# The end of a mixture-of-experts layer: only the last expert is split, in two halves, and TensorE adds the last shift of one token block

## The chip, the cores and the metric

The kernel runs on one core of one Trainium2 chip. The core has five engines with their own queues: TensorE (PE; its weight loads are listed apart as PEld), VectorE (DVE), ScalarE (ACT), GpSimd (POOL) and SyncE (SP), which here issues the transfers. The metric is the device time of one execution in microseconds, median of several; lower is better. TensorE's clock has two levels, 1.2 and 2.4 GHz, shown as a granted clock of 0.5 and 1.0.

## The reference

One transformer layer over 256 latent tokens of 1024 channels: a mixer (attention and pooling), a layer norm, and then the part that matters here, a mixture of 32 experts in 4 groups, two experts per token:

```python
for g in range(N_GROUPS):
    a = jnp.einsum('td,edf->tef', ht, w_gate[sl])
    u = jnp.einsum('td,edf->tef', ht, w_up[sl])
    act = jax.nn.silu(a) * u * gates[:, sl, None]
    y = y + jnp.einsum('tef,efd->td', act, w_down[sl])
...
h_new = layer_norm(alpha * h_new + gate2 * y, ln2_g, ln2_b)
```

All is float32. Each expert has a gate and an up matrix of 1024 x 512 and a down matrix of 512 x 1024, 2 MB each, 6 MB per expert.

## The kernel before

**Weights.** From about 190 us on the kernel streams the 32 experts through 20 slots of 1 MB in SBUF, taken in a fixed round (`wtile`, line 867). SP issues one transfer after the other (line 877 for gate and up in four, line 886 for down in two); a slot's new transfer waits until the products that read the old tile are done. Load calls run two experts ahead.

**One expert.** Up to 32 tokens of an expert stand as 32 columns. `gate_up` (line 816) multiplies them by gate and up, 8 steps `k` of 8 products into one PSUM tile `gue`; ACT takes the SiLU (line 827), DVE multiplies (line 833), and `turn` (line 836) transposes to `aTe`. `down` (line 841) makes 16 products of 256 columns into `ye`, and DVE multiplies by `g2b` into the expert's 32 rows of `yp` (line 850). This runs inside the next expert's `gate_up`, ahead of its step 2. Four experts fill the 128 rows of `yp`; then four products of 512 columns with `OTg` (`close_group`) add the rows to the tokens in `ya`, four PSUM tiles: two token blocks by two column halves. Each product of the program stands as two MATMUL records in the trace.

**Order.** Tile's scheduler may move instructions, except where `tc.keep_in_program_order` pins them: `pin` does that for products while `pinned[0]` is set, `fx` for others.

**The end before.** The last two experts, 30 and 31, are treated apart (`last_two`, line 960). Both experts' gate and up come first, then both down matrices in eight pieces of 256 columns, 512 KB each (`PIECES`, `parts`), interleaved so that pieces of 30 run ahead of those of 31. The layer norm's rows `l2` are loaded after all of that (line 1012), and POOL spreads them to all partitions (line 942). After gate and up of expert 31, `piece` (line 1047) makes 16 products of 64 columns and four DVE multiplications per piece; `gather` (line 1060) adds 256 finished columns to both token blocks, and a finished half gets its statistics (line 1066). Then, per token block i and half d (lines 1088 to 1116): `first` subtracts the mean and multiplies by the norm's gain; `second` scales by the reciprocal deviation and adds the shift, for block 0 by ACT and POOL (lines 1096, 1097), for block 1 by one DVE instruction (line 1099); four transfers of 256 KB write the result (line 1103).

Of the kernel before, what the change touches and what calls it, by code (L numbers as in the profile page):

```python
# [8 lines left out]
F32 = mybir.dt.float32  # L9
# [12 lines left out]
NE = 32  # L22
# [5 lines left out]
EPS = 1e-5  # L28
NEG = -1e30
WINS = (2, 4, 8, 16)  # L30
PIECES = ((0, 256, 512, 768, 1024), (0, 256, 512, 768, 1024))


@with_exitstack
def block_kernel(ctx, tc, x, cx, cols, rows, gate_bias, bands, w_mod, w_in, bias, w_grp, w_attn, w_pool, w_out,
# [14 lines left out]
    def two(name):  # L50
        return ps.tile([P, 512], F32, tag="two", bufs=2, name=name)

    def tmpb(name):
        return ps.tile([P, 512], F32, tag="tmp", bufs=2, name=name)
# [9 lines left out]
    def fx(ins):  # L64
        return tc.keep_in_program_order(ins) if early[0] else ins
# [709 lines left out]
    def mm(*a, **k):  # L775
        return pin(nc.tensor.matmul(*a, **k))  # L776
# [90 lines left out]
    def wtile(shape, name):  # L867
        r, t = order[slot[0] % 20]
        slot[0] += 1
        return r.tile(shape, F32, tag=t, name=name)  # L870

    def load_gate_up(e):
        ts = []
        for q in range(4):
            t = wtile([P, 4, 512], f"wgu{e}_{q}")
            w = (w_gate, w_up)[q % 2]
            nc.sync.dma_start(t, w[e].rearrange("(a p b) f -> a p b f", a=2, b=4)[q // 2])
            ts.append(t)
        return lambda k: [ts[k // 4 * 2 + s][:, k % 4, :] for s in range(2)]
# [65 lines left out]
    def first_residual():  # L945
        r = wtile([P, 2, D], "res")
        l1 = two_rows(2, "l1")
        for i in range(2):
# [4 lines left out]
            V.scalar_tensor_tensor(o, l1[:, 1], ALPHA, o, op0=OP.mult, op1=OP.add)  # L953
        return r

    parts = sorted(((i, a, b) for i in range(2) for a, b in zip(PIECES[i], PIECES[i][1:])),
                   key=lambda t: (t[1] // 256 + t[0] * 1.5, t[1]))
    loaded, groups, acts, outs = {}, {}, {}, {}

    def last_two(e):  # L960
        for i in range(2):
            loaded[e + i] = (load_gate_up(e + i), {})
        for i, a, b in parts:
            wds = loaded[e + i][1]
            if a % 512 == 0:
                wds[a // 512] = wtile([P, 4, 512], f"wd{e + i}_{a // 512}")
            nc.sync.dma_start(wds[a // 512][:, :, a % 512:a % 512 + b - a],
                              w_down[e + i].rearrange("(p k) f -> p k f", k=4)[:, :, a:b])

    def load_ahead(e):  # L970
        if e < NE - 2:
            loaded[e] = (load_gate_up(e), load_down(e))
        elif e == NE - 2:
            last_two(e)

    def open_group(g):
        outs[g] = (spread_back(groups[g][1], 0, P, f"g{g}"), M.tile([P, D], F32, tag="yp", bufs=1, name=f"yp{g}"))
# [29 lines left out]
    for e in range(NE):  # L1007
        if e == OV - 1:
            res = first_residual()
        load_ahead(e + 2)  # L1010
        if e == NE - 4:
            l2 = two_rows(4, "l2")
        last = e >= NE - 2
        pinned[0] = e < 1 or last
        g, j = e // EG, e % EG

        def mid(k):
            if e == 0 and k % 2 == 0:
                step(k // 2)
            if e - 1 in acts_in and e - 1 < NE - 2 and k == 2:  # L1020
                old_work(e - 1)
            if e == NE - 1 and k == 2:
                acts[e - 1] = turn(acts_in.pop(e - 1), f"e{e - 1}")

        acts_in[e] = gate_up(groups[g][0], CAP * j, loaded[e][0], f"e{e}", mid)
        if j == EG - 2 and e < NE - EG and e != OV - 1:
            dispatch_next(g + 1)
        if e == OV:
            old_work(e)
            most = nc.values_load(cnt[0:1, NE:NE + 1], min_val=0, max_val=T)  # L1030
            with tc.If(most > CAP):
                was, pinned[0] = pinned[0], False
                overflow()
                pinned[0] = was
            dispatch_next(g + 1)
        if e == OV + 1:
            for i in range(2):
                for d in range(2):
                    mm(ya[i][d], lhsT=ident, rhs=res[:, i, 512 * d:512 * d + 512], start=False,
                                     stop=False)  # L1040
# [2 lines left out]
    OT, yp = outs[NE // EG - 1]  # L1043
    fx = tc.keep_in_program_order
    stats = [M.tile([P, 2, 6], F32, name=f"fst{i}", bufs=1) for i in range(2)]

    def piece(n, e, c, w):
        y = (two, tmpb)[n // 2 % 2](f"yl{n}")
        wd = loaded[NE - 2 + e][1][c // 512]
        for f in range(4):  # L1050
            for d in range(4):
                o = c % 512 + w * d
                mm(y[32 * d:32 * d + 32, 0:w], lhsT=acts[NE - 2 + e][:, f, :], rhs=wd[:, f, o:o + w],
                   start=f == 0, stop=f == 3)
        p = 64 + 32 * e
        for d in range(4):
            o = slice(c + w * d, c + w * d + w)
            fx(V.tensor_mul(yp[p:p + 32, o], y[32 * d:32 * d + 32, 0:w], g2b[32 * d:32 * d + 32, o]))  # L1058

    def gather(c0, c1):  # L1060
        for i in range(2):
            t = ya[i][c0 // 512]
            mm(t[:, c0 % 512:c0 % 512 + c1 - c0], lhsT=OT[:, P * i:P * i + P], rhs=yp[:, c0:c1], start=False,
               stop=c1 % 512 == 0)
            if c1 % 512 == 0:
                fx(V.bn_stats(stats[i][:, c0 // 512, :], t))  # L1066

    ready = []
    for n, (i, a, b) in enumerate(parts):
        piece(n, i, a, (b - a) // 4)  # L1070
        if n == 0:
            acts[NE - 1] = turn(acts_in.pop(NE - 1), f"e{NE - 1}")
        while ready:
            gather(*ready.pop(0))
        if i:
            ready.append((a, b))
    gather(*ready.pop(0))
    l2g, l2b = l2[:, 0], l2[:, 1]


    fin = keep.tile([P, 2, D], F32, tag="k16", name="fin")
# [1 line left out]
    for i in range(2):  # L1083
# [1 line left out]
        fx(V.bn_aggr(mv[:, 0:2], flat(stats[i])))  # L1085
        nc.scalar.activation(mv[:, 2:3], mv[:, 1:2], AF.Sqrt, bias=epst, scale=1.0)
        mvs.append(mv)
    def first(i, d):
        cs = slice(512 * d, 512 * d + 512)
        fx(V.scalar_tensor_tensor(fin[:, i, cs], ya[i][d], mvs[i][:, 0:1], l2g[:, cs], op0=OP.subtract, op1=OP.mult))  # L1090

    def second(i, d):
        cs = slice(512 * d, 512 * d + 512)
        f = fin[:, i, cs]
        if i == 0:
            fx(nc.scalar.activation(f, f, AF.Copy, scale=mvs[i][:, 3:4]))
            fx(nc.gpsimd.tensor_add(f, f, l2b[:, cs]))
        else:
            fx(V.scalar_tensor_tensor(f, f, mvs[i][:, 3:4], l2b[:, cs], op0=OP.mult, op1=OP.add))

    def write(i, d):
        cs = slice(512 * d, 512 * d + 512)
        fx(nc.sync.dma_start(out[P * i:P * i + P, cs], fin[:, i, cs]))

    for i in range(2):
        for d in range(2):
            first(i, d)
            if d == 0:
                fx(V.reciprocal(mvs[i][:, 3:4], mvs[i][:, 2:3]))
            if i == 0:  # L1110
                second(i, d)
    for d in range(2):
        second(1, d)
    for d in range(2):
        for i in range(2):
            write(i, d)


# [57 lines left out]
```

## Time and profile before

| | |
|---|---|
| median of 3 runs | 732.76 us (732.16 to 733.72) |
| profiled execution | 733.38 us, its span 731.7 us |
| busy in the span | PE 78%, PEld 59%, DVE 43%, ACT 21%, POOL 2% |
| mean granted TensorE clock | 0.867 |
| moved by DMA | 260.09 MB, mean 355 GB/s |

The span runs from the first to the last instruction; times in rows are microseconds from its start. The page gives the span in 40 slices of 18.3 us. From slice 18 to 38 the DMA digit is 9 and the rate 415 to 420 GB/s; the last two slices have 311 and 70 GB/s. A row "[0.71 <-DMA wd...]" says that the engine stood idle for 0.71 us and what ended that; "issue" is idle time that ended with nothing the profile shows.

### The profile page before, as it was taken

How to read it: one execution, taken by the hardware profiler on the slowest of the kernel's cores; microseconds unless marked ns; L12 is line 12 of the kernel's file. 1: busy time of each engine (PE TensorE's matmuls, PEld its weight loads, DVE VectorE, ACT ScalarE, POOL GpSimd, SP SyncE). 2: the span in 40 equal slices, each digit the busy share in tenths (PEclk: the TensorE clock that was granted, in tenths of full speed). 3: DMA queues.
4: the chain of work that ended last, by engine and by line, in shares of the span. 5: the costliest groups of instructions: out<-in, count | busy, mean ns of one | idle time of the engine just before them, and what ended most of it. 6: DMA issues, size and time to landing. Idle time of an engine off the chain costs nothing.

```text
span 731.7 us, 16776 instructions
## 1 busy us (share of the span) xinstructions
PE 570.9 (78%) x7373; PEld 429.5 (59%) x7374; DVE 316.5 (43%) x778; ACT 156.1 (21%) x305; POOL 17.4 (2%) x39
## 2 busy tenths in 40 slices
PE   7898999999999989885767756668576659757462
PEld 5787666599997757664355434446334427634341
DVE  5669947979658554332122113112112332312126
ACT  4333455555545441010000001001000001100011
POOL 1000000000000030000000000000000010000003
PEclk9999999999999969997876869777785787979788
DMA  9999764789987749999999999999999999999991
GB/s 292 309 347 386 270 176 158 265 312 349 354 309 312 261 157 385 416 417 418 419 418 420 417 419 420 417 418 417 419 417 419 420 415 417 416 418 419 418 311 70
DMA packets 69628, 260.09 MB, mean 355 GB/s; under 512 B 6568, under 2 KB 27560, under 8 KB 45228
## 3 DMA queue, kind: packets, MB, share of 16 engines
q1 hardware_dynamic: 69550, 258.97, 90.9%
q8 instruction: 59, 0.97, 0.5%
q14 instruction: 19, 0.16, 0.1%
HBM read 257.90 MB, written 1.05 MB: 354 GB/s over the span
## 4 chain that ended last, share of the span: by engine, by line
DMA 52%; issue 36%; PE 8%; DVE 3%; POOL 0%; DVEq 0%; ACT 0%; SPq 0%; POOLq 0%
DMA wgu<-in_w_expert_up_dram 28%; DMA wd<-in_w_expert_down_dram 17%; DMA wgu<-in_w_expert_gate_dram 8%; PE gue L776 4%; PE ye L776 1%; PE pdd L776 1%; PE ya L776 1%; DVE yp L1058 0%; DVE se L684 0%; PE yl L776 0%; DVE fst L1066 0%; DVEq L1172 0%; DVE fin L1090 0%; DVE eq L684 0%; DVE spe L833 0%
## 5 line engine op out<-in xcount | busy, mean ns | idle before, releaser
L776 PE MATMUL gue<-wgu,xgd 128*32 128x128 f32 x4096 | 173.3, 329 | 82.5 <-DMA wgu<-in_w_expert_up_dram 52.5
L776 PEld LDWEIGHTS gue<-wgu,xgd 128*32 128x32 f32 x4096 | 138.5, 132 | 120.1 <-DMA wgu<-in_w_expert_up_dram 63.8
L776 PE MATMUL ye<-wd,aTe 128*32 128x256 f32 x960 | 73.3, 435 | 32.7 <-DVE aTe L838 15.7
L850 DVE TENSOR_TENSOR yp<-ye,g2b 32x256 f32<-32x256 f32 x120 | 50.4, 420 | 100.1 <-PE ye L776 98.7
L833 DVE TENSOR_TENSOR spe<-gue,sie 128x128 f32<-128x128 f32 x32 | 12.0, 375 | 161.8 <-ACT sie L827 161.6
L827 ACT ACTIVATE sie<-gue 128x128 f32<-128x128 f32 x32 | 8.9, 277 | 335.6 <-PE gue L776 335.6
L776 PEld LDWEIGHTS ye<-wd,aTe 128*32 128x32 f32 x960 | 32.4, 121 | 60.8 <-issue 17.7
L776 PE MATMUL pdd<-OHd,hx 128*128 128x128 f32 x256 | 41.7, 315 | 3.4 <-DVE yp L850 3.0
L776 PEld LDWEIGHTS pdd<-OHd,hx 128*128 128x128 f32 x256 | 37.0, 223 | 11.7 <-issue 5.8
L776 PE MATMUL ya<-yp,OTg 128*128 128x512 f32 (+1 forms) x72 | 33.4, 598 | 7.1 <-DVE yp L850 5.2
L362 DVE SCALAR_TENSOR_TENSOR ms<-wr,sil,ms 128x512 f32<-128x512 f32 x42 | 36.9, 878 | 0.2
L806 DVE TENSOR_SCALAR xgd<-pdd,G2c,B2c 128x128 f32<-128x128 f32 x32 | 13.1, 410 | 48.3 <-PE pdd L776 48.1
L804 ACT ACTIVATE xgd<-pdd,B2c,G2c 128x128 f32<-128x128 f32 x32 | 14.6, 457 | 84.3 <-DVE xgd L806 80.7
L776 PEld LDWEIGHTS ya<-yp,OTg 128*128 128x128 f32 x72 | 12.7, 199 | 22.4 <-DVE yp L850 13.2
L414 ACT ACTIVATE sb<-sb,mx 128x512 f32<-128x512 f32 x16 | 11.5, 719 | 10.3 <-DVE mx L413 10.1
L859 DVE COPY OTg<-potg 128x256 f32<-128x256 f32 x8 | 3.4, 424 | 23.0 <-PE ya L776 14.0
L423 PE MATMUL ptt<-ident,sb 128*128 128x128 f32 x64 | 10.2, 284 | 2.9 <-DVE yaT L69 2.7
L423 PEld LDWEIGHTS ptt<-ident,sb 128*128 128x128 f32 x64 | 6.8, 140 | 7.2 <-DVE yaT L69 5.3
L469 PEld LDWEIGHTS po<-pT,kv 128*64 128x64 f32 x128 | 7.4, 136 | 5.6 <-issue 3.3
L838 DVE STREAM_TRANSPOSE aTe<-spe 128x128 f32<-128x128 f32 x32 | 10.0, 312 | 1.1
L942 POOL PARTITION_BROADCAST l<-l1r x4 | 2.8, 798 | 318.3 <-DMA l1r<-in_rows_dram 318.3
L400 PE MATMUL s<-kv,qT 64*128 64x512 f32 x32 | 10.1, 640 | 0.3 <-DVE mx L412 0.3
(851 smaller groups left out, 971.4 us busy)
## 6 DMA issues: line engine op xcount, KB each, us to landing
wgu<-in_w_expert_gate_dram SPq DMA_DIRECT2D x64, 1024.0 KB, 19.9
wgu<-in_w_expert_up_dram SPq DMA_DIRECT2D x64, 1024.0 KB, 20.5
wd<-in_w_expert_down_dram SPq DMA_DIRECT2D x60, 1024.0 KB, 19.9
wr<-in_w_mod_dram SPq DMA_DIRECT2D x16, 1024.0 KB, 6.6
wm<-in_w_mod_dram SPq DMA_DIRECT2D x16, 512.0 KB, 7.9
wg<-in_w_in_dram SPq DMA_DIRECT2D x8, 1024.0 KB
wq<-in_w_in_dram SPq DMA_DIRECT2D x8, 512.0 KB, 8.3
wo<-in_w_out_dram SPq DMA_DIRECT2D x4, 1024.0 KB, 8.8
```

The source lines that it names most:

```text
L362: V.scalar_tensor_tensor(o, v, sil[:, k + j, 0:1], o, op0=OP.mult, op1=OP.add)
L400: ins = nc.tensor.matmul(ss[r], lhsT=qT[hr, c, P * tt:P * tt + P], rhs=kT[hr, c, :], start=True, stop=True)
L414: nc.scalar.activation(sb, sb, AF.Exp, bias=mx[:, 2:3], scale=1.0, accum_out=mx[:, 3:4])
L423: nc.tensor.transpose(pt[:, P * j:P * j + P], sb[:, P * j:P * j + P], ident)
L469: ins = nc.tensor.matmul(po[64 * r:64 * r + 64, 0:P], lhsT=vr[:, j, 128 * m + 64 * r:128 * m + 64 * r + 64], rhs=pTs[i - 1 + r][:, j, :], ...
L776: return pin(nc.tensor.matmul(*a, **k))
L804: nc.scalar.activation(xg[:, k, :], src, AF.Identity, bias=B2c[:, k:k + 1], scale=G2c[:, k:k + 1])
L806: V.tensor_scalar(xg[:, k, :], src, G2c[:, k:k + 1], B2c[:, k:k + 1], op0=OP.mult, op1=OP.add)
L827: nc.scalar.activation(si, gu[:, 0, :], AF.Silu)
L833: V.tensor_mul(sp.rearrange("p (k r) -> p k r", k=4), by_four(gu[:, 1, :]), by_four(si))
L838: V.transpose(flat(aT), si)
L850: V.tensor_mul(yp[32 * par:32 * par + 32, 256 * d:256 * d + 256], y[32 * d:32 * d + 32, 0:256], g2b[32 * d:32 * d + 32, 256 * d:256 * d + ...
```

## The change

Expert 30 loses its special treatment: its down matrix comes in the usual two transfers, ahead of gate and up of expert 31, and its down products run inside `gate_up` of expert 31. It is no longer pinned. Expert 31's down matrix comes in two halves of 512 columns, 1 MB each (`load_last`); per half there are 16 products of 128 columns, four DVE multiplications, and products of 512 columns into both token blocks. The rows `l2` are loaded ahead of expert 30. For token block 0 a product of `ident` with the shift fills a PSUM tile `fo` early (`shift`); at the end a diagonal matrix `dg` of the reciprocal deviations, made by ACT, multiplies the half into the same tile, and ACT copies it out. POOL no longer takes part at the end. One line less at the head of the file moves all line numbers by one.

```diff
-    def last_two(e):
-        for i in range(2):
-            loaded[e + i] = (load_gate_up(e + i), {})
-        for i, a, b in parts:
...
+    def load_last(e):
+        gu, ts = load_gate_up(e), []
+        for d in range(2):
+            t = wtile([P, 4, 512], f"wd{e}_{d}")
+            nc.sync.dma_start(t, w_down[e].rearrange("(p k) f -> p k f", k=4)[:, :, 512 * d:512 * d + 512])
+            ts.append(t)
+        return gu, ts
...
-        load_ahead(e + 2)
         if e == NE - 4:
             l2 = two_rows(4, "l2")
-        last = e >= NE - 2
+        load_ahead(e + 2)
+        last = e == NE - 1
...
+    fos = [two(f"fo{d}") for d in range(2)]
+    def shift(d):
+        fx(nc.tensor.matmul(fos[d], lhsT=ident, rhs=l2b[:, 512 * d:512 * d + 512], start=True, stop=False))
+    def gather(d):
+        for i in range(2):
+            mm(ya[i][d], lhsT=OT[:, P * i:P * i + P], rhs=yp[:, 512 * d:512 * d + 512], start=False, stop=True)
+            fx(V.bn_stats(stats[i][:, d, :], ya[i][d]))
+    aT = turn(acts_in.pop(NE - 1), f"e{NE - 1}")
+    for h in range(2):
+        y = tmpb(f"yl{h}")
+        shift(h)
+        wd = loaded[NE - 1][1][h]
+        for f in range(4):
             for d in range(4):
...
+                mm(y[32 * d:32 * d + 32, 0:P], lhsT=aT[:, f, :], rhs=wd[:, f, P * d:P * d + P], start=f == 0,
+                   stop=f == 3)
...
+        gather(h)
...
-            fx(nc.scalar.activation(f, f, AF.Copy, scale=mvs[i][:, 3:4]))
-            fx(nc.gpsimd.tensor_add(f, f, l2b[:, cs]))
...
+                    fx(nc.scalar.activation(dg, ident, AF.Copy, scale=mvs[0][:, 3:4]))
+                fx(nc.tensor.matmul(fos[d], lhsT=dg, rhs=part(0, d), start=False, stop=True))
...
+        fx(nc.scalar.copy(part(0, d), fos[d]))
```

SP's queue at the end, before: `wgu` are gate and up, of expert 31 in the first four rows; `wd_0_7710` and `wd_1_7715` are the down matrix of expert 30, `wd_0_7713` and `wd_1_7719` that of 31.

```order
L877 DMA wgu_0_7702<-in_w_expert_gate_dram 128x2048
L877 DMA wgu_1_7704<-in_w_expert_up_dram 128x2048
L877 DMA wgu_2_7706<-in_w_expert_gate_dram 128x2048
L877 DMA wgu_3_7708<-in_w_expert_up_dram 128x2048
L967 DMA wd_0_7710<-in_w_expert_down_dram 128x4x256 x2
L967 DMA wd_0_7713<-in_w_expert_down_dram 128x4x256
L967 DMA wd_1_7715<-in_w_expert_down_dram 128x4x256
L967 DMA wd_0_7713<-in_w_expert_down_dram 128x4x256
L967 DMA wd_1_7715<-in_w_expert_down_dram 128x4x256
L967 DMA wd_1_7719<-in_w_expert_down_dram 128x4x256 x2
L938 DMA l2r<-in_rows_dram 1x2048
```

The same place of the change: `wd_0_7709` and `wd_1_7711` are the down matrix of expert 30, then gate and up of 31, and its two halves.

```order
L885 DMA wd_0_7709<-in_w_expert_down_dram 128x2048
L885 DMA wd_1_7711<-in_w_expert_down_dram 128x2048
L876 DMA wgu_0_7809<-in_w_expert_gate_dram 128x2048
L876 DMA wgu_1_7811<-in_w_expert_up_dram 128x2048
L876 DMA wgu_2_7813<-in_w_expert_gate_dram 128x2048
L876 DMA wgu_3_7815<-in_w_expert_up_dram 128x2048
L961 DMA wd_0_7817<-in_w_expert_down_dram 128x4x512
L961 DMA wd_1_7819<-in_w_expert_down_dram 128x4x512
```

The 2 MB of expert 30's down matrix moved from behind to ahead of expert 31's gate and up; `l2r` stands further up, ahead of expert 30.

TensorE's queue from the end of expert 31's gate and up to its last product, before (`yl` are the pieces; with `aTe_8032` of expert 30, with `aTe_8109` of 31):

```order
L776 MATMUL gue_8015<-wgu_3_7708,xgd_7543 32x128 x4
L776 MATMUL yl_8088<-wd_0_7710,aTe_8032 32x64 x16
L776 MATMUL yl_8111<-wd_0_7710,aTe_8032 32x64 x16
L776 MATMUL yl_8132<-wd_0_7713,aTe_8109 32x64 x16
L776 MATMUL yl_8153<-wd_1_7715,aTe_8032 32x64 x16
L776 MATMUL ya_2868<-yp_7849,OTg_7847 128x256
L776 MATMUL ya_2870<-yp_7849,OTg_7847 128x256
L776 MATMUL yl_8176<-wd_0_7713,aTe_8109 32x64 x16
L776 MATMUL yl_8197<-wd_1_7715,aTe_8032 32x64 x16
L776 MATMUL ya_2868<-yp_7849,OTg_7847 128x256
L776 MATMUL ya_2870<-yp_7849,OTg_7847 128x256
L776 MATMUL yl_8222<-wd_1_7719,aTe_8109 32x64 x16
```

The same place of the change, to the end:

```order
L775 MATMUL gue_8011<-wgu_3_7815,xgd_7543 32x128 x4
L1043 MATMUL fo_8105<-l_7695,ident 128x512
L775 MATMUL yl_8109<-wd_0_7817,aTe_8107 32x128 x16
L775 MATMUL ya_2868<-yp_7845,OTg_7843 128x512
L775 MATMUL ya_2870<-yp_7845,OTg_7843 128x512
L1043 MATMUL fo_8106<-l_7695,ident 128x512
L775 MATMUL yl_8135<-wd_1_7819,aTe_8107 32x128 x16
L775 MATMUL ya_2869<-yp_7845,OTg_7843 128x512
L775 MATMUL ya_2871<-yp_7845,OTg_7843 128x512
L1086 MATMUL fo_8105<-fin,dg 128x512
L1086 MATMUL fo_8106<-fin,dg 128x512
```

The second half's products now stand behind the first half's products into `ya` and behind the second fill; expert 30's down products left this place.

They stand in the middle of expert 31's gate and up, in the change (`ye_8030`):

```order
L775 MATMUL gue_8011<-wgu_0_7809,xgd_7543 32x128 x4
L775 MATMUL gue_8011<-wgu_1_7811,xgd_7543 32x128 x4
L775 MATMUL gue_8011<-wgu_0_7809,xgd_7543 32x128 x4
L775 MATMUL gue_8011<-wgu_1_7811,xgd_7543 32x128 x4
L775 MATMUL ye_8030<-wd_0_7709,aTe_8028 32x256 x8
L775 MATMUL ye_8030<-wd_1_7711,aTe_8028 32x256 x8
L775 MATMUL gue_8011<-wgu_0_7809,xgd_7543 32x128 x4
L775 MATMUL gue_8011<-wgu_1_7811,xgd_7543 32x128 x4
```

Before, expert 29's down products stood at this place of expert 30, and none in expert 31; in the change those of 29 stand ahead of all of expert 30's.

## Rows read from the trace of the kernel before

**Rows 1.** The page, shares of the span in the chain that ended last.
```profile
DMA 52%; issue 36%; PE 8%; DVE 3%; POOL 0%; DVEq 0%; ACT 0%; SPq 0%; POOLq 0%
```
**Rows 2.** Timeline of SP: start, us, line, transfer, count.
```profile
678.11 0.33 SPq L877 DMA_DIRECT2D wgu<-in_w_expert_up_dram  x1
681.42 0.33 SPq L877 DMA_DIRECT2D wgu<-in_w_expert_gate_dram  x1
683.74 0.33 SPq L877 DMA_DIRECT2D wgu<-in_w_expert_up_dram  x1
686.25 22.82 SPq L967 DMA_DIRECT2D wd<-in_w_expert_down_dram  x8
```
**Rows 3.** The down tiles from 640 us: issue duration min/median/max in ns.
```profile
L967 SPq DMA_DIRECT2D wd<-in_w_expert_down_dram x8: 541/1358/8861, 686.2 to 707.7; - x8
```
**Rows 4.** Stretches: length, busy time by engine, then granted clock, DMA share, GB/s.
```profile
58.00:78.00 20.00, 18.09 (x135) 14.49 (x134) 18.78 (x47) 7.81 (x15) 0.00 (x0) 1.00 1.05 387
640.00:690.00 50.00, 26.89 (x514) 18.35 (x518) 7.52 (x19) 0.83 (x3) 0.00 (x0) 0.83 1.01 419
704.50:712.00 7.50, 5.89 (x186) 5.08 (x187) 3.70 (x16) 1.56 (x2) 0.00 (x0) 0.79 1.01 323
```
**Rows 5.** Timeline of TensorE: start, us, product, records, idle before and its releaser.
```profile
661.67 3.74 PE L776 MATMUL ya<-yp,OTg 128*128 128x512 f32 x8 [0.29 <-DVE yp L850]
688.72 1.51 PE L776 MATMUL gue<-wgu,xgd 128*32 128x128 f32 x24 [1.75 <-DMA wgu<-in_w_expert_up_dram]
690.00 3.64 PE L776 MATMUL ye<-wd,aTe 128*32 128x256 f32 x32
693.41 3.07 PE L776 MATMUL gue<-wgu,xgd 128*32 128x128 f32 x96
699.46 1.98 PE L776 MATMUL gue<-wgu,xgd 128*32 128x128 f32 x56 [1.99 <-DMA wgu<-in_w_expert_up_dram]
704.46 3.21 PE L776 MATMUL gue<-wgu,xgd 128*32 128x128 f32 x56 [1.86 <-DMA wgu<-in_w_expert_up_dram]
715.71 0.63 PE L776 MATMUL yl<-wd,aTe 128*32 128x64 f32 x26 [2.02 <-issue]
```
**Rows 6.** One-us stretches where the granted clock changed (third number from the end).
```profile
693.00:694.00 1.00, 1.00 (x20) 0.74 (x16) 0.29 (x1) 0.00 (x0) 0.00 (x0) 0.51 1.05 434
707.00:708.00 1.00, 1.00 (x48) 0.95 (x37) 0.00 (x0) 0.26 (x1) 0.00 (x0) 0.69 0.98 295
724.00:725.00 1.00, 0.00 (x0) 0.00 (x0) 1.00 (x2) 1.00 (x2) 0.30 (x1) 0.85 0.00 0
```
**Rows 7.** Timeline of all engines at the end.
```profile
707.74 0.28 ACT L827 ACTIVATE sie<-gue 128x128 f32<-128x128 f32 x1 [10.90 <-PE gue L776]
708.46 0.31 DVE L838 STREAM_TRANSPOSE aTe<-spe 128x128 f32<-128x128 f32 x1
722.64 0.28 DVE L1085 BATCH_NORM_AGGREGATE fmv<-fst 128x2 f32<-128x12 f32 x2
723.83 1.37 ACT L1096 ACTIVATE fin<-fin,fmv 128x512 f32<-128x512 f32 x2 [0.46 <-DVE fmv L1109]
```
**Rows 8.** DVE from 690 us, shapes apart: count, busy us, mean ns, idle before.
```profile
L1058 DVE TENSOR_TENSOR yp<-yl,g2b 32x64 f32<-32x64 f32 x32 | 7.1, 222 | 3.3 <-PE yl L776 2.9
L1066 DVE BATCH_NORM_STATS2 fst<-ya 128x6 f32<-128x512 f32 x4 | 2.6, 691 | 0.8 <-PE ya L776 0.8
L850 DVE TENSOR_TENSOR yp<-ye,g2b 32x256 f32<-32x256 f32 x4 | 1.7, 419 | 12.8 <-PE ye L776 12.8
```
**Rows 9.** The output's tiles: ns min/median/max, first and last start.
```profile
L1099 DVE SCALAR_TENSOR_TENSOR fin<-fin,fmv,l x2: 787/1266/1746, 725.7 to 726.4; 128x512 f32<-128x512 f32 x2
L1103 SPq DMA_DIRECT2D out_dram<-fin x4: 332/336/374, 726.0 to 728.2; - x4
```
**Rows 10.** Stretches of 1 us while the result is written.
```profile
727.00:728.00 1.00, 0.00 (x0) 0.00 (x0) 1.00 (x1) 0.00 (x0) 0.64 (x1) 0.50 1.04 391
729.00:730.00 1.00, 0.00 (x0) 0.00 (x0) 0.00 (x0) 0.00 (x0) 0.00 (x0) 0.50 0.91 342
```

More of the change, by code (lines that the diff above doesn't have):

```diff
@@ L30 @@
 WINS = (2, 4, 8, 16)
-PIECES = ((0, 256, 512, 768, 1024), (0, 256, 512, 768, 1024))
 @with_exitstack
@@ L954, in first_residual @@
         return r
-    parts = sorted(((i, a, b) for i in range(2) for a, b in zip(PIECES[i], PIECES[i][1:])),
-                   key=lambda t: (t[1] // 256 + t[0] * 1.5, t[1]))
     loaded, groups, acts, outs = {}, {}, {}, {}
-    def last_two(e):
-        for i in range(2):
-            loaded[e + i] = (load_gate_up(e + i), {})
-        for i, a, b in parts:
[L964 to L968, printed above, removed]
+    def load_last(e):
[5 more added lines that the diff above has]
+        return gu, ts
     def load_ahead(e):
-        if e < NE - 2:
+        if e < NE - 1:
             loaded[e] = (load_gate_up(e), load_down(e))
-        elif e == NE - 2:
-            last_two(e)
+        elif e == NE - 1:
+            loaded[e] = load_last(e)
     def open_group(g):
@@ L1019, in mid @@
                 step(k // 2)
-            if e - 1 in acts_in and e - 1 < NE - 2 and k == 2:
+            if e - 1 in acts_in and k == 2:
                 old_work(e - 1)
-            if e == NE - 1 and k == 2:
-                acts[e - 1] = turn(acts_in.pop(e - 1), f"e{e - 1}")
         acts_in[e] = gate_up(groups[g][0], CAP * j, loaded[e][0], f"e{e}", mid)
@@ L1045, in block_kernel @@
     stats = [M.tile([P, 2, 6], F32, name=f"fst{i}", bufs=1) for i in range(2)]
-    def piece(n, e, c, w):
-        y = (two, tmpb)[n // 2 % 2](f"yl{n}")
-        wd = loaded[NE - 2 + e][1][c // 512]
+    l2g, l2b = l2[:, 0], l2[:, 1]
+    fos = [two(f"fo{d}") for d in range(2)]
[10 more added lines that the diff above has]
+        wd = loaded[NE - 1][1][h]
         for f in range(4):
             for d in range(4):
[L1052 to L1055, printed above, removed]
+                mm(y[32 * d:32 * d + 32, 0:P], lhsT=aT[:, f, :], rhs=wd[:, f, P * d:P * d + P], start=f == 0,
+                   stop=f == 3)
         for d in range(4):
[L1057 to L1078, printed above, removed]
+            o = slice(512 * h + P * d, 512 * h + P * d + P)
+            fx(V.tensor_mul(yp[96:128, o], y[32 * d:32 * d + 32, 0:P], g2b[32 * d:32 * d + 32, o]))
+        gather(h)
     fin = keep.tile([P, 2, D], F32, tag="k16", name="fin")
@@ L1087, in block_kernel, with part @@
         mvs.append(mv)
[L1088 to L1095, printed above, removed]
-            fx(nc.scalar.activation(f, f, AF.Copy, scale=mvs[i][:, 3:4]))
-            fx(nc.gpsimd.tensor_add(f, f, l2b[:, cs]))
[L1098 to L1103, printed above, removed]
+    dg = M.tile([P, P], F32, name="dg", bufs=1)
+    def part(i, d):
+        return fin[:, i, 512 * d:512 * d + 512]
     for i in range(2):
         for d in range(2):
-            first(i, d)
+            fx(V.scalar_tensor_tensor(part(i, d), ya[i][d], mvs[i][:, 0:1], l2g[:, 512 * d:512 * d + 512],
+                                      op0=OP.subtract, op1=OP.mult))
             if d == 0:
@@ L1110, in block_kernel @@
             if i == 0:
-                second(i, d)
+                if d == 0:
+                    fx(nc.scalar.activation(dg, ident, AF.Copy, scale=mvs[0][:, 3:4]))
+                fx(nc.tensor.matmul(fos[d], lhsT=dg, rhs=part(0, d), start=False, stop=True))
     for d in range(2):
-        second(1, d)
+        fx(nc.scalar.copy(part(0, d), fos[d]))
+        fx(V.scalar_tensor_tensor(part(1, d), part(1, d), mvs[1][:, 3:4], l2b[:, 512 * d:512 * d + 512], op0=OP.mult,
+                                  op1=OP.add))
     for d in range(2):
         for i in range(2):
-            write(i, d)
+            fx(nc.sync.dma_start(out[P * i:P * i + P, 512 * d:512 * d + 512], part(i, d)))
 def kernel(**inputs):
```

## The prediction

> **What bounds the kernel now.** I read the page first, then the queue of SP, then stretches with their rates, then TensorE's timeline, and the end last. On the page the chain that ended last is mostly DMA [rows 1]; the reader is to see that the stream of weights, and no engine, sets when expert 31 can start. SP's rows show the pace, since a new transfer is issued when an older one has landed: 3.3, 2.3 and 2.5 us lie between these four [rows 2]; the rate agrees, 1.049 MB at 419 GB/s is 2.50 us for each MB [rows 4]. The last stretch is different. The eight pieces of the down matrices lie in rows of 1 KB; SP was held for 8.86 us in issuing one of them [rows 3], and the rate fell to 323 GB/s although the engines were busy [rows 4]. So the pieces do cost bandwidth.
>
> Three moments then tell the rest. The last MB of expert 31's gate and up is there at 704.46, where TensorE starts its last 56 records, after a wait for it [rows 5]. Their result reaches ACT at 707.74, which I call E; the statistics of the layer norm are complete at 722.64, which I call A [rows 7]. From E to A is 14.90 us, all of it a serial pass through pieces, and from A to the end of the span (731.7) it is 9.06 us. The profiled execution took 733.38 us, 1.68 us outside its span, and lies 0.62 us above the median of 732.76; I work in the span and carry the difference to the median.
>
> **The change, step by step: when E comes.** Everything up to expert 30 keeps its amount of bytes and its order; `l2r` is 8 KB further up and costs 0.02 us by the rate. Expert 30's two down transfers now go ahead of expert 31's gate and up: 2 x 2.50 = 5.0 us later for each of the four. The second MB was there at 699.46 [rows 5], now at 704.46; the fourth at 709.46. From the second MB on TensorE has 24 records, then expert 30's down (32 records), then 96 records less what waits for the last MB. Expert 30 did the same work before: it started at 688.72 and its 96 records ended at 693.41 + 3.07 = 696.48 [rows 5], 7.76 us. That gives 712.2. In that stretch the clock rose from 1.2 to 2.4 GHz at about 694.0, 5.3 us after the work began; at expert 31 it rose about 707.3, 2.85 us after 704.46 [rows 6]. With the early rise TensorE is done with all else by 709.46 and only the 56 records after the last MB remain: at the rate of 3.07 us for 96 they take 1.8 us, 711.3. I take the middle, E = 711.75, 4.0 us later than before.
>
> **From E to A.** SiLU, multiplication and transpose: 708.46 + 0.31 - 707.74 = 1.03, with the handover 1.08 [rows 7]. The first fill product lies in this gap: two records of 512 columns, 0.9 us, with TensorE otherwise idle and its tile and the shift long there, so it costs nothing; without the gap it costs 0.87. The half's 16 products are 32 records of 128 columns, a third of the 96: 1.02 + 0.05. Four multiplications of 128 columns are not in the trace; between 0.222 us at 64 and 0.419 at 256 [rows 8] a line gives 0.29, four with gaps 1.20. Eight records of 512 columns took 3.74 [rows 5], so a product takes 0.87 behind another and about 0.94 alone: the first half into `ya` takes 0.05 + 1.74 until TensorE is free. Then, queued behind it in the same order, the second fill 0.87, the second half's products 1.07, and its multiplications 1.20. Last the second half into `ya`: 0.05 + 0.94 + 0.87 for the second token block, 0.05, and 0.69 for its statistics [rows 8], 2.60. Sum: 1.08 + 1.07 + 1.20 + 1.79 + 0.87 + 1.07 + 1.20 + 2.60 = 10.9 us against 14.9. What this saves is four of eight pieces on the serial path and the stall of 2.02 us in the middle of a piece [rows 5]. Both halves' transfers must be there: with rows of 2 KB the stretch from 58 to 78 us moved 387 GB/s [rows 4], 2.71 us each, so 712.2 and 714.9 against a need at 712.8 and about 717.8. The first has 0.6 us of cover; what it is late goes straight into A. A = 711.75 + 10.9 = 722.65, the same as before.
>
> **From A to the end.** Before, POOL's addition lies beside DVE's last two instructions, and these took 0.787 and 1.746 us [rows 9]. Without POOL both should take 0.79, and the last write is issued 0.95 us earlier. But the four writes of 256 KB move one behind the other: 391 GB/s in one stretch and still 342 in the last [rows 10]; 1.05 MB at 391 is 2.68 us, and the first was issued at 726.00, the last at 728.2 [rows 9]. So the first write counts as much as the last. It now waits for: `dg` after the reciprocal at A + 1.19 (ACT starts there before, too [rows 7]) 0.28, the product 0.99, the copy 0.69 + 0.05, so A + 3.20 instead of A + 3.36. Bounds: if only the last issue counts, 0.95 less; if the clock has fallen by then, the product takes 0.87 more and the end comes 0.7 later. It fell at about 724.85 [rows 6]; TensorE's last record ended one statistic (0.69) and a handover ahead of A, at 721.9, so 2.95 us passed. In the change the product starts at A + 1.5, 2.25 us after the last record, so I take it as fast: 0.16 us from the first write, a little from the last, 0.3 us less in all.
>
> **Sum.** E + 4.0, E to A - 4.0, the end - 0.3: span 731.4, the profiled execution 733.1, on the median basis 732.76 - 0.3, about 732.5 us.
>
> A rule of the Trainium skill speaks for more at this point: the page "DMA: Bandwidth & Descriptors", section "Anatomy of one DMA", gives each transfer a fixed part of some 2.0 us plus its bytes over the bandwidth. By that rule the end follows the last issue and the sum would be 0.65 us lower, 730.75 in the span; the rows of the writes, which move back to back, speak for the smaller gain.
>
> **Rivals.** A measurement of this kernel can tell about 0.2%, 1.5 us, from no change.
>
> Faster: the gap of 3.3 us in place of 2.5 between two landings [rows 2] need not come again, so the last MB may be there at 708.65; with the early rise of the clock E is 710.45, 1.3 less. With the writes following the last issue another 0.65: span 729.45 to 730.1, 730.5 to 731.2 on the median basis. For it speaks that the gap is one of three distances shown and that rows of 1 KB disturb the stream no more; against it that it needs the early rise of the clock too, and of the two seen one was late.
>
> Slower, by the clock: expert 30's down products now stand inside expert 31's gate and up. At 1.2 GHz they take 3.4 us (3.64 with the tail of the last record [rows 5]), and the 120 other records at 3.21 us for 56 take 6.9. All at the lower clock E is 704.46 + 10.3 = 714.7, 3.0 later: span 734.4, 735.5 on the median basis. From rows it decides from the point where the clock rises later than 7.2 us after 704.46 (E = 709.6 + half of that time, 713.2); 2.85 and 5.3 were seen.
>
> Slower, by a stall of TensorE: before, 2.02 us passed in the middle of a piece with nothing that the profile shows [rows 5]. In the change all that follows E hangs on TensorE's order, so one such stall goes to the end in full: span 733.4, 734.5 on the median basis. For it: the products come as densely as then. Against: there are about half as many of them at the end, and SP no longer pushes pieces of 1 KB.
>
> Slower, by landings: one more gap of 0.8 us and a first half that needs 3.2 instead of 2.71 us add 1.0 to 1.6, 734 us at the most.
>
> **How the numbers follow.** The forecast 58%; faster 20%; clock 8%; stall 10%; landings 4%. The last three make 22% slower, though a part of the stall and of the landings stays below 0.2%, as a part of the faster case does on its side. The forecast's own range is 731.3 to 734.0. To leave out no more than two in ten I go down to 730.6 (nearly all of the faster case) and up to 735.0, above the stall and below the whole clock case.
>
> **What would show it.** Right: the last `wgu` wait of TensorE ends near 709.5, E near 711.8, no wait of TensorE for the halves, statistics complete near 722.7, DVE's last two instructions at 0.79 us each, first write near A + 3.2. Wrong: E before 710.5 or after 713, an idle stretch of TensorE with "issue" behind E, a wait for `wd` of expert 31, or writes that end with the last issue and not with the first.

## The result, and the profile after

The change is slower: 739.43 us median of 8 runs (738.80 to 740.87) against 733.29 (730.47 to 737.53) for the kernel before beside it, ratio 1.0075 with a 95% interval of 1.0053 to 1.0097. (A ratio with its interval is taken over all runs and need not be the quotient of the two medians.) The profiled execution took 740.87 us, the slowest of the eight; its span is 739.2 us, 7.5 more than that of before. Between the medians the loss is 6.1 us.

Most of it is lost before the first weight matters. The start of the change in the timeline, engines POOL, PE and SP (start, us, line, operation, idle before and its releaser):

```profile
1.12 0.20 POOL L95 MEMSET ones<- 128x128 f32 x1
9.52 0.60 POOL L86 TENSOR_SCALAR_AFFINE_SELECT ident<-ident 128x128 f32<-128x128 f32 x1 [8.20 <-issue]
10.53 0.31 POOL L104 MEMSET zeros<- 128x256 f32 x1
10.88 8.47 PE L265 MATMUL warm<-zeros,ones 128*128 128x256 f32 x24 [10.88 <-POOL zeros L104]
...
91.05 0.35 SPq L484 DMA_DIRECT2D band<-in_bands_dram  x1
...
194.20 0.50 SPq L876 DMA_DIRECT2D wgu<-in_w_expert_gate_dram  x1
```

The same instructions before, and two of the end that are needed below:

```profile
1.62 0.29 POOL L87 TENSOR_SCALAR_AFFINE_SELECT ident<-ident 128x128 f32<-128x128 f32 x1 [0.29 <-POOL ones L96]
2.30 0.31 POOL L105 MEMSET zeros<- 128x256 f32 x1
2.67 8.02 PE L266 MATMUL warm<-zeros,ones 128*128 128x256 f32 x24 [2.67 <-POOL zeros L105]
...
84.56 0.35 SPq L485 DMA_DIRECT2D band<-in_bands_dram  x1
...
187.79 0.50 SPq L877 DMA_DIRECT2D wgu<-in_w_expert_gate_dram  x1
...
724.70 2.94 POOL L1097 TENSOR_TENSOR fin<-fin,l 128x512 f32<-128x512 f32 x2 [8.36 <-ACT fin L1096]
...
726.00 2.55 SPq L1103 DMA_DIRECT2D out_dram<-fin  x4
```

GpSimd stands still for 8.20 us with "issue", that is, nothing in this view releases it, in front of an instruction that the change does not touch. TensorE's first products wait for its `zeros` and come 8.21 us later (10.88 against 2.67), the load of `band` 6.49, the first expert's weights 6.41. The 1.7 us regained in between were not isolated.

The chain on the page still is mostly DMA, as in [rows 1]:

```profile
DMA 56%; issue 35%; PE 5%; DVE 2%; POOL 0%; DVEq 0%; SPq 0%; ACT 0%; POOLq 0%
```

The end of the change, timeline of all engines; it answers to [rows 5] and [rows 7 to 9]:

```profile
711.07 1.51 PE L775 MATMUL gue<-wgu,xgd 128*32 128x128 f32 x24 [1.75 <-DMA wgu<-in_w_expert_up_dram]
712.36 3.64 PE L775 MATMUL ye<-wd,aTe 128*32 128x256 f32 x32
715.77 3.28 PE L775 MATMUL gue<-wgu,xgd 128*32 128x128 f32 x96
...
718.98 1.13 PE L1043 MATMUL fo<-l,ident 128*128 128x512 f32 x2
719.13 0.28 ACT L826 ACTIVATE sie<-gue 128x128 f32<-128x128 f32 x1 [14.48 <-PE gue L775]
...
720.22 1.08 PE L775 MATMUL yl<-wd,aTe 128*32 128x128 f32 x32
721.37 1.20 DVE L1061 TENSOR_TENSOR yp<-yl,g2b 32x128 f32<-32x128 f32 x4 [1.20 <-PE yl L775]
722.62 1.98 PE L775 MATMUL ya<-yp,OTg 128*128 128x512 f32 x4 [1.32 <-DVE yp L1061]
...
724.44 1.02 PE L1043 MATMUL fo<-l,ident 128*128 128x512 f32 x2
...
725.39 1.08 PE L775 MATMUL yl<-wd,aTe 128*32 128x128 f32 x32
726.54 1.20 DVE L1061 TENSOR_TENSOR yp<-yl,g2b 32x128 f32<-32x128 f32 x4 [1.20 <-PE yl L775]
727.79 1.98 PE L775 MATMUL ya<-yp,OTg 128*128 128x512 f32 x4 [1.32 <-DVE yp L1061]
...
730.54 0.28 DVE L1069 BATCH_NORM_AGGREGATE fmv<-fst 128x2 f32<-128x12 f32 x2
...
732.18 1.98 PE L1086 MATMUL fo<-fin,dg 128*128 128x512 f32 x4 [2.40 <-ACT dg L1085]
...
733.34 0.58 ACT L1088 COPY fin<-fo 128x512 f32<-128x512 f32 x1 [1.22 <-PE fo L1086]
733.63 1.41 DVE L1089 SCALAR_TENSOR_TENSOR fin<-fin,fmv,l 128x512 f32<-128x512 f32 x2
733.95 1.83 SPq L1093 DMA_DIRECT2D out_dram<-fin  x4
```

E is 719.13, A is 730.54. So E is 11.39 us later than before, E to A takes 11.41 instead of 14.90 (3.49 less), and A to the end of the span 8.66 instead of 9.06 (0.40 less): +7.50. The second MB of expert 31's gate and up was forecast for 704.46 and came at 711.07, 6.61 later. With this 6.6 taken off, E is 4.8 later than before and the whole tail costs 0.9 us.

The stretches that answer to [rows 4], [rows 6] and [rows 10], in the same columns:

```profile
711.00:718.00 7.00, 6.93 (x120) 4.86 (x124) 1.69 (x4) 0.00 (x0) 0.00 (x0) 0.59 0.66 251
716.00:717.00 1.00, 1.00 (x28) 0.94 (x24) 0.91 (x3) 0.00 (x0) 0.00 (x0) 0.62 0.52 184
735.00:736.00 1.00, 0.00 (x0) 0.00 (x0) 0.04 (x1) 0.00 (x0) 0.00 (x0) 1.00 1.02 381
736.00:737.00 1.00, 0.00 (x0) 0.00 (x0) 0.00 (x0) 0.00 (x0) 0.00 (x0) 1.00 1.02 379
```

The clock rose within 716 to 717, about 5.7 us after the work began at 711.07; the writes again move back to back.

### The profile page after: what moved, and what is told of

It reads as the page before. It is cut to its first block, busy times and chain, and to the rows that moved or that the text cites. A ratio compares the mean times of both kernels' runs of the same rounds, so it can differ in the third digit from the quotient of the medians.

```text
span 739.2 us, 16427 instructions
## 1 busy us (share of the span) xinstructions
PE 561.2 (76%) x7213; PEld 420.1 (57%) x7214; DVE 312.5 (42%) x758; ACT 156.0 (21%) x306; POOL 14.8 (2%) x37
## 2 busy tenths in 40 slices
DMA packets 66746, 260.07 MB, mean 352 GB/s; under 512 B 6504, under 2 KB 23400, under 8 KB 42092
## 4 chain that ended last, share of the span: by engine, by line
DMA 56%; issue 35%; PE 5%; DVE 2%; POOL 0%; DVEq 0%; SPq 0%; ACT 0%; POOLq 0%
DMA wgu<-in_w_expert_up_dram 31%; DMA wd<-in_w_expert_down_dram 17%; DMA wgu<-in_w_expert_gate_dram 8%; PE gue L775 3%; PE pdd L775 1%; PE ye L775 1%; PE ya L775 1%; DVE oh L718 0%; DVE yp L1061 0%; PE yl L775 0%; DVE fin L1079 0%; DVE eq L683 0%; DVEq L1149 0%; PE fo L1043 0%; DVE spe L832 0%
## 5 line engine op out<-in xcount | busy, mean ns | idle before, releaser
L775 PE MATMUL gue<-wgu,xgd 128*32 128x128 f32 x4096 | 168.2, 321 | 88.7 <-DMA wgu<-in_w_expert_up_dram 60.7
L775 PEld LDWEIGHTS gue<-wgu,xgd 128*32 128x32 f32 x4096 | 135.0, 129 | 126.2 <-DMA wgu<-in_w_expert_up_dram 72.5
L849 DVE TENSOR_TENSOR yp<-ye,g2b 32x256 f32<-32x256 f32 x124 | 52.1, 420 | 99.7 <-PE ye L775 98.3
L775 PE MATMUL ya<-yp,OTg 128*128 128x512 f32 x64 | 32.7, 643 | 7.9 <-DVE yp L849 5.2
L775 PEld LDWEIGHTS ya<-yp,OTg 128*128 128x128 f32 x64 | 11.1, 197 | 23.0 <-DVE yp L849 12.7
L265 PE MATMUL warm<-zeros,ones 128*128 128x256 f32 x24 | 8.5, 534 | 10.9 <-POOL zeros L104 10.9
L265 PEld LDWEIGHTS warm<-zeros,ones 128*128 128x128 f32 x24 | 6.6, 280 | 12.0 <-POOL zeros L104 10.6
```

The lines of the kernel that those rows point to most:

```text
L265: tc.keep_in_program_order(nc.tensor.matmul(t[:, 0:256], lhsT=ones, rhs=zeros, start=True, stop=True))
L849: V.tensor_mul(yp[32 * par:32 * par + 32, 256 * d:256 * d + 256], y[32 * d:32 * d + 32, 0:256], g2b[32 * d:32 * d + 32, 256 * d:256 * d + ...
```

## Why GpSimd stands still: theory and rivals

On GpSimd's queue, the order of instructions has a row `ISA` that carries no tile, wherever ordinary work follows partition broadcasts or the other way round. The end of the queue before:

```
L942 ISA l_7723<-l2r 128x512 x4
L1097 ISA
L1097 TENSOR_TENSOR fin<-fin,l_7723 128x512 x2
```

and in the change:

```
L941 ISA l_7695<-l2r 128x512 x4
```

Both programs also have such a row ahead of the first AFFINE_SELECT.

The timelines above leave it out, but the trace has it: the view of a source line shows it on GpSimd's queue as `MODIFY_POOL_CONFIG` (duration min/median/max in ns, first and last start in us). The first two lines are of before, at its start and at its end, the third is of the start of the change:

```profile
L87 POOLq MODIFY_POOL_CONFIG  x2: 11/11/11, 1.5 to 1.6; - x2
L1097 POOLq MODIFY_POOL_CONFIG  x2: 127/127/127, 716.3 to 716.3; - x2
L86 POOLq MODIFY_POOL_CONFIG  x2: 11/11/11, 1.3 to 1.4; - x2
```

At the start both kernels have the same row, and only in the change 8 us pass behind it: its AFFINE_SELECT starts at 9.52, that of before at 1.62. At the end of before the row stands right behind the last partition broadcast (713.58 to 716.35), 8.4 us ahead of the additions.

**Theory.** After a partition broadcast GpSimd must be set up again for ordinary instructions, some 7 to 8 us, and it keeps what it was last set up for into the next execution. Before, POOL's last additions made it do that near the end, in the 8.36 us in which it waited for ACT anyway (the row of 724.70). The change removed those additions, so the next execution does it first, on the path. **Rivals:** the start is an accident of the profiled execution, or comes from the split, the loads or the fill products; or what counts is that some ordinary GpSimd work follows a broadcast anywhere, or merely that GpSimd ends early.

## The experiments

Times of the kernel before beside them: 734.24 us for the first four, 734.20 for the others; ratios are to it, with 95% intervals.

| run | us | ratio | POOL's first AFFINE_SELECT |
|---|---|---|---|
| e1_pool_op_last | 734.88 | 1.0026 [0.9999, 1.0053] | 1.62 |
| e2_before_no_pool_add | 741.05 | 1.0086 [1.0062, 1.0110] | 9.70 |
| e3_pool_op_between | 740.16 | 1.0090 [1.0062, 1.0118] | 9.57 |
| e4_split_only | 733.11 | 0.9983 [0.9953, 1.0012] | 1.62 |
| e5_end_only | 733.08 | 0.9996 [0.9971, 1.0022] | 1.62 |
| e6_halves_first | 731.93 | 0.9976 [0.9953, 1.0000] | 1.62 |
| e7_halves_first_old_end | 731.51 | 0.9965 [0.9949, 0.9981] | 1.62 |
| e8_no_broadcast | 738.88 | 1.0069 [1.0046, 1.0093] | 1.38 |

**1. The change with one small addition last on GpSimd** (one column, its result unused):

```diff
             l2 = two_rows(4, "l2")
+            pz = M.tile([P, 1], F32, name="pz", bufs=1)
+            nc.gpsimd.tensor_add(pz, l2[:, 1, 1022:1023], l2[:, 1, 1023:1024])
```

> The changed kernel plus one addition of 128x1 on GpSimd behind the broadcast of l2; its result is not used. Theory one (left-over state): the 8.2 us that GpSimd stands still ahead of its first select at the start are a reload, needed because the last GpSimd work of the execution before was a broadcast; with an ordinary addition last, the stall at the start goes, the stream of weights starts 6.6 us earlier, and the time is 739.4 - 6.6 = 732.8, within 1 us. The 8 us then show between the broadcast of l2 and the new addition, where nobody waits for GpSimd. Rival (the stall belongs to the changed program as such, its layout or its instruction fetch): 739.4, stall of 8.2 us at the start as before.

734.88 us. GpSimd in its timeline:

```profile
1.62 0.29 POOL L86 TENSOR_SCALAR_AFFINE_SELECT ident<-ident 128x128 f32<-128x128 f32 x1 [0.29 <-POOL ones L95]
...
675.78 2.77 POOL L941 PARTITION_BROADCAST l<-l2r  x4 [87.09 <-DMA wd<-in_w_expert_down_dram]
685.70 0.18 POOL L1008 TENSOR_TENSOR pz<-l 128x1 f32<-128x1 f32 x1 [7.14 <-issue]
```

The standstill has moved: 7.14 us lie between the broadcast and the addition, where nobody waits, and none at the start. The time is 2.1 us above the 732.8 that was expected "within 1 us", so the size was missed: the expectation took 6.6 us from the profiled executions, and that of the change was the slowest of its eight. The kernel before stood at 733.29 us beside the change and stands at 734.24 here. Between the two medians the addition brought 4.55 us, between the two profiled spans 6.1 (739.2 and 733.1), and the first expert's weights are asked for at 188.15 in place of 194.20.

**2. The kernel before without GpSimd's additions** (block 0 scaled and shifted by DVE, as block 1):

```diff
-        if i == 0:
-            fx(nc.scalar.activation(f, f, AF.Copy, scale=mvs[i][:, 3:4]))
-            fx(nc.gpsimd.tensor_add(f, f, l2b[:, cs]))
-        else:
-            fx(V.scalar_tensor_tensor(f, f, mvs[i][:, 3:4], l2b[:, cs], op0=OP.mult, op1=OP.add))
+        fx(V.scalar_tensor_tensor(f, f, mvs[i][:, 3:4], l2b[:, cs], op0=OP.mult, op1=OP.add))
```

> The kernel before, with the two additions of GpSimd at the end taken away: token block 0 gets its scale and shift by one DVE instruction per half, as block 1 does. Nothing else of the change is in it. Theory one (left-over state): the last GpSimd work is the broadcast of l2, so the start stalls for 8.2 us and the time rises by 6.6 us for that; the end itself, two DVE instructions of 0.79 us more and one of 1.75 us back at 0.79, costs about 0.5: 740.4. Rival (the stall belongs to the changed program as such): 733.8, no stall at the start.

741.05 us. The pieces and loads of before are all there, and so is the standstill:

```profile
9.70 0.50 POOL L87 TENSOR_SCALAR_AFFINE_SELECT ident<-ident 128x128 f32<-128x128 f32 x1 [8.37 <-issue]
...
719.23 2.77 POOL L942 PARTITION_BROADCAST l<-l2r  x4 [125.79 <-PE yl L776]
```

So it comes from neither the split nor the fill products.

**3. The same addition between the two broadcasts** of `l1` and `l2` in place of behind the second:

```diff
+        if i == 2:
+            pz = M.tile([P, 1], F32, name="pz", bufs=1)
+            nc.gpsimd.tensor_add(pz, t[:, 1, 1022:1023], t[:, 1, 1023:1024])
```

> The changed kernel plus one addition of 128x1 on GpSimd behind the broadcast of l1, that is ahead of that of l2; its result is not used. Theory one (left-over state): the last GpSimd work is still a broadcast, so the start stalls for 8.2 us as in the changed kernel: 739.4. Rival (it is enough that GpSimd does some ordinary work late in the program, or any other instruction that moves the layout): no stall, 732.8.

740.16 us. The same instruction as in 1, once more ordinary work behind a broadcast, but with a broadcast last:

```profile
9.57 0.54 POOL L86 TENSOR_SCALAR_AFFINE_SELECT ident<-ident 128x128 f32<-128x128 f32 x1 [8.24 <-issue]
...
600.66 0.18 POOL L944 TENSOR_TENSOR pz<-l 128x1 f32<-128x1 f32 x1 [7.37 <-DMA wgu<-in_w_expert_gate_dram]
680.58 2.80 POOL L941 PARTITION_BROADCAST l<-l2r  x4 [79.73 <-DMA l2r<-in_rows_dram]
```

It pays twice, 7.37 us behind the first broadcasts (which end at 593.29; the row `MODIFY_POOL_CONFIG` of line 944 stands at 593.2, and the DMA named as releaser is only the last event before the addition) and 8.24 us at the start. Only the one at the start shows in the time. What stands last decides: runs 1 and 3 differ in nothing but the place of the addition, and their medians by 5.3 us.

**4. The split alone**: the change with the end of before (ACT and POOL for block 0, no `fo`, no `dg`).

```diff
-        shift(h)
...
-                if d == 0:
-                    fx(nc.scalar.activation(dg, ident, AF.Copy, scale=mvs[0][:, 3:4]))
-                fx(nc.tensor.matmul(fos[d], lhsT=dg, rhs=part(0, d), start=False, stop=True))
+                second(i, d)
```

> The change without its new end: expert 31 split in two halves, expert 30 whole, l2 loaded early, but no fill products, and block 0 finished by ACT and GpSimd as before. Theory one (left-over state): an addition of GpSimd is last, so no stall at the start; what is left is the price of the split. In the profile of the changed kernel the statistics are complete 7.9 us later than before, 6.6 of these from the start, so 1.3 us for the split, less 0.9 for the second fill product, which is gone: 733.3 + 0.4 = 733.7. Rival (the stall belongs to the changed loads or the split): 739.4 to 740.

733.11 us, no difference from before. POOL's additions start right when ACT's result is there; their `MODIFY_POOL_CONFIG` stands at 678.3, behind the early broadcasts of `l2` and 46 us ahead of them. TensorE's second half follows the first gather without a fill:

```profile
704.11 1.51 PE L775 MATMUL gue<-wgu,xgd 128*32 128x128 f32 x24 [1.75 <-DMA wgu<-in_w_expert_up_dram]
...
710.24 1.74 PE L775 MATMUL gue<-wgu,xgd 128*32 128x128 f32 x56 [1.00 <-DMA wgu<-in_w_expert_up_dram]
712.04 0.28 ACT L826 ACTIVATE sie<-gue 128x128 f32<-128x128 f32 x1 [14.93 <-PE gue L775]
...
715.52 1.98 PE L775 MATMUL ya<-yp,OTg 128*128 128x512 f32 x4 [1.32 <-DVE yp L1055]
...
717.44 1.08 PE L775 MATMUL yl<-wd,aTe 128*32 128x128 f32 x32
...
722.59 0.28 DVE L1063 BATCH_NORM_AGGREGATE fmv<-fst 128x2 f32<-128x12 f32 x2
...
724.65 2.95 POOL L1075 TENSOR_TENSOR fin<-fin,l 128x512 f32<-128x512 f32 x2 [46.26 <-ACT fin L1074]
```

E to A is 10.55 us against 11.41 in run 1 (712.82 to 724.23), which differs in this by the second fill: from the first half's products into `ya` to the second half's 1.92 us here (715.52 to 717.44), 2.78 in run 1 (716.30 to 719.08).

**5. The new end alone**, with the pieces of before; the fills behind the last product into `ya`, the addition of run 1 on GpSimd.

```diff
+    for d in range(2):
+        fx(nc.tensor.matmul(fos[d], lhsT=ident, rhs=l2b[:, 512 * d:512 * d + 512], start=True, stop=False))
...
-            first(i, d)
+            fx(V.scalar_tensor_tensor(part(i, d), ya[i][d], mvs[i][:, 0:1], l2g[:, 512 * d:512 * d + 512],
+                                      op0=OP.subtract, op1=OP.mult))
...
-                second(i, d)
+                fx(nc.tensor.matmul(fos[d], lhsT=dg, rhs=part(0, d), start=False, stop=True))
```

> The kernel before with its pieces kept, and only the end of the change: TensorE adds the shift of token block 0 with fill products that stand behind the last product into ya, ACT copies out; a one-column POOL addition behind the spread of l2 keeps GpSimd's last work an ordinary instruction. Theory (the new end is worth -0.3 to +0.4 us, no more): 733.5 to 734.6 us beside 734.2 for the kernel before. Rival (the end as a whole costs what the change lost, the start is only its place in the record): 739 us or more.

733.08 us, 0.4 below the expected range, but the interval holds 1: the end by TensorE is worth nothing that these runs can tell. From A to the end of its span are 8.93 us (724.67 to 733.6) against 9.06 before.

**6 and 7. Both halves' products ahead of the products into `ya`**, in 6 with the change's end and run 1's addition, in 7 with the end of before. On TensorE the second half no longer stands behind the first gather, which waits for DVE's multiplications.

```diff
                 fx(V.tensor_mul(yp[96:128, o], y[32 * d:32 * d + 32, 0:P], g2b[32 * d:32 * d + 32, o]))
+    for h in range(2):
         gather(h)
```

> The change with the one-column POOL addition, and on TensorE both halves' products (and both fills) ahead of the products of 512 columns into ya. Theory (what is left from E to A is a serial chain, TensorE waits for DVE's multiplications and the second half waits behind the first half's gather): about 2 us less than the change with the POOL addition alone, 732.9 against 734.9 us, E to A about 9.3 instead of 11.4 us; about 1 us of the possible 3 is kept back by the landing of the second half, for which TensorE now waits. Rival (the second half lands too late for it): 734.5 to 735 us, the gain turned into a wait for wd of expert 31.

> The split alone (the end of before with ACT and POOL, no fill products) with both halves' products ahead of the products of 512 columns into ya. Theory: about 2 us less than the split alone, 731.1 against 733.1 us, E to A about 8.5 instead of 10.55 us, and no standstill of GpSimd at the start, since POOL's additions stand at the end. Rival (the second half lands too late): 732.8 to 733.2 us with a wait of TensorE for wd of expert 31.

731.93 and 731.51 us. Run 7, TensorE and E and A:

```profile
705.11 1.51 PE L775 MATMUL gue<-wgu,xgd 128*32 128x128 f32 x24 [1.74 <-DMA wgu<-in_w_expert_up_dram]
...
713.19 0.28 ACT L826 ACTIVATE sie<-gue 128x128 f32<-128x128 f32 x1 [14.51 <-PE gue L775]
...
714.28 1.08 PE L775 MATMUL yl<-wd,aTe 128*32 128x128 f32 x32 [1.16 <-DVE aTe L837]
...
715.83 1.08 PE L775 MATMUL yl<-wd,aTe 128*32 128x128 f32 x32 [0.47 <-DMA wd<-in_w_expert_down_dram]
...
716.84 3.70 PE L775 MATMUL ya<-yp,OTg 128*128 128x512 f32 x8
...
721.31 0.28 DVE L1064 BATCH_NORM_AGGREGATE fmv<-fst 128x2 f32<-128x12 f32 x2
```

E to A takes 8.12 us instead of 10.55, in run 6 8.64 (715.29 to 723.93) instead of 11.41. In run 7 TensorE waits 0.47 us for the second half, so the landing is the next bound. The wait of about 1 us expected in run 6 is not there: TensorE makes the second fill in that time. Run 7 is the one version here whose interval lies below 1. The steps from run 4 to 7 and from run 1 to 6 are each less sure than E to A makes them: the intervals of 4 and 7 overlap, those of 1 and 6 just touch.

**8. The change without any partition broadcast**: the rows `l1` and `l2` come to all partitions by transfers.

```diff
-        r, t = wtile([P, 2, D], name + "r"), wtile([P, 2, D], name)
-        nc.sync.dma_start(r[0:1], rows[:, D * i:D * i + 2 * D])
...
+        t = wtile([P, 2, D], name)
+        nc.sync.dma_start(t.rearrange("p a b -> p (a b)"), rows[:, D * i:D * i + 2 * D].to_broadcast([P, 2 * D]))
```

> The change, but the four rows of the two norms come to all partitions by broadcasting transfers instead of GpSimd's partition broadcasts; about 2 MB more are written into SBUF. Theory (the standstill at the start is GpSimd changing back from what the partition broadcasts left): without any partition broadcast it never changes, the first affine_select starts below 2 us, and the time is 739.4 - 6.6 + up to 5 for the extra traffic, 733 to 738 us. Rival (POOL merely ends too early, whatever it did last): the standstill of 8.2 us stays, 739 to 744 us.

738.88 us. The time alone decides nothing: it is above the range of the one and at the lower edge of the other. The profile does:

```profile
1.38 0.29 POOL L86 TENSOR_SCALAR_AFFINE_SELECT ident<-ident 128x128 f32<-128x128 f32 x1
```

GpSimd's last instruction in this run ends at 265.8 us, earlier than anywhere else, and there is no standstill: ending early is not the cause. The first expert's weights are asked for at 186.87 against 188.15 us in run 1, yet the second MB of expert 31's gate and up is there only at 708.66 against 705.34: the stream lost 4.6 us to 2.1 MB more (262.15 against 260.07 MB), near what these take at the stream's pace [rows 4].

**What follows.** All rivals fell: the standstill follows what stood last on GpSimd in all nine kernels with broadcasts and is gone without them. It is 7.14 to 8.37 us behind a row `MODIFY_POOL_CONFIG`, and no instruction fills it. The page "GPSIMD Engine Reference" of the Trainium skill, section "Instruction dispatch", says that the first call to a freshly loaded GpSimd kernel pays about 6 us that no profile instruction shows; the traces agree that no instruction fills the time, though the row ahead of it is there, and measure 1.1 to 2.4 us more. The page "Runtime: NRT & Kernel Launch", section "nrt_init cost", says that a kernel on a runtime kept open starts from what the one before it left; it names SBUF, event flags and HBM and not GpSimd's code, and runs 1 and 3 agree as far as GpSimd goes. That it is carried over was inferred from programs whose start is the same and whose end differs; a first execution, or one behind another kernel, was not looked at.

## Why the prediction was wrong

**The step that failed** is the end without POOL: "Without POOL both should take 0.79, and the last write is issued 0.95 us earlier." The part that it named is right: DVE's last two took 1.41 us together, and SP was done with the writes at 735.78, A + 5.24, where it was at 728.55, A + 5.91, before. But taking POOL away was counted only where POOL had been. Its 8.36 us of idle time ahead of line 1097 looked like a wait for ACT and hid a second wait of 7 to 8 us; the removed row `ISA` ahead of these additions stood in the order of the instructions, and its row at 716.3 in the trace of before. The price came on the opposite end of the kernel, and none of the rivals had it: 6.4 us at the first expert's weights in the profiled executions, 5.3 us between the medians of runs 3 and 1.

**When E comes.** The bytes were right: the second MB came at the forecast's time plus the late start, to 0.2 us. The term from there to E was too small, 8.06 us in place of 7.29. The middle between early and late rise of the clock was taken, as if only one of them could hold E back. In the change the rise was late, and E went by TensorE's work, for which the prediction had 712.2, that is 7.74. In run 4 the clock rose early (about 3.0 us after 704.11), and E still came 7.93 us behind the second MB, because the last MB landed at 710.24, 6.1 us behind it and not 5.0; runs 1, 6 and 7 gave 7.48, 7.94 and 8.08. In run 4 the rate fell in that stretch from 393 GB/s (704 to 705 us) to 184 (709 to 710): the last MB did not come at the 2.50 us for each MB that the forecast gave it. The rivals had such a delay only as a gap like that of [rows 2], which lies in mid-stream; that the stream thins out at its end belongs into the forecast. One reading of [rows 6] was off, too, without moving the sum: between levels of 0.5 and 1.0 a mean of 0.69 puts the rise of before at 707.6, 3.2 us after 704.46, and not at 707.3, and 0.85 puts the fall at 724.7.

**From E to A** the mechanism was right and the sum 0.5 low, 11.41 for 10.9. The handovers make it: multiplications 1.25 with the step to the next engine (1.20 taken), products of a half 1.15 (1.07), the last gather with both statistics 2.75 (2.60), the fill 0.95 (0.87). The first fill does lie in the gap ahead of the transpose: 1.09 us from E to the first half in the change, 1.09 in run 4 without fills. The second costs 0.86 us on the path (runs 1 and 4), as said.

**From A to the end** 0.40 was gained for 0.3, and that it fits is luck. The first write came at A + 3.41 and not 3.20 (`dg` 0.40 us for 0.28, the product until its copy starts 1.16 for 0.99), the last issue was done 0.67 earlier; the end moved by an amount between the two. But with the end of before A to the end is 9.06, 8.91 (run 4) and 8.89 (run 7), and with the end of the change 8.66, 8.93 (run 5), 8.87 (run 1), 9.07 (runs 3 and 6) and 9.28 (run 8): no gain stands clear of that spread. In runs 1, 3, 6 and 8 the closing products took 2.79 to 3.25 us in place of 1.98, since the granted clock fell to 0.5 while they ran (in run 1 from 0.96 in the stretch of 726 us to 0.50 in that of 727). The prediction had this as a bound, "the product takes 0.87 more", and took it as not coming. The rule of the Trainium skill that it weighs there stands in a section on transfers that GpSimd issues, while SP issues these writes; of the 0.65 us more that it would give, the profiled execution shows 0.1.

**The rivals.** No idle stretch with "issue" of TensorE behind E, no wait for the halves, the clock's rise below the 7.2 us that the clock rival needed. The change's own work, without the standstill, is run 1: 734.88 us, 0.6 above the median of before where 0.3 below was forecast; its interval (0.9999 to 1.0053) does not tell it from no change. It lies inside the stated range of 730.6 to 735.0, at its upper end.

## What to carry to other kernels

Before taking work off an engine, read what its last instruction leaves behind for the next execution, and compare the orders of the instructions for rows without a tile that vanish: idle time that ends with another engine can hide a second wait. An "issue" standstill in front of an instruction that nobody touched was here the sign that the engine started from another state. And where a serial tail alternates between two engines, put the work that depends on neither ahead of the first wait: here this was worth 2.4 to 2.8 us from E to A, and 1.6 to 3.0 us between the medians, the smaller of which is not clear of the noise.

## What the runs showed of the hardware

GpSimd took 7.14 to 8.37 us from partition broadcasts to the next ordinary instruction, behind a row `MODIFY_POOL_CONFIG` of 11 to 127 ns, each time that it went from the one to the other: twice in run 3, and also, by the inference above, when the two lie in different executions. What the way from ordinary work to broadcasts takes was not seen, since GpSimd stood idle there for 79.73 us (run 3) or more. While the last transfers (the end of gate and up, and the two halves of the last down matrix) came in, with nothing queued behind them, the DMA engines were busy for half the time (0.52 and 184 GB/s in the stretch from 716 us), where the stretch of rows of 2 KB in [rows 4] moved 387 GB/s; why was not tried. The granted clock rose 3.0 (run 4) to 5.8 us (run 7) after TensorE's work on the second MB of expert 31 began, in kernels whose products there are the same.
